# Empty bytes ahead of tiles in a four-layer trunk kernel: where streamed and held rows of matmuls begin modulo 256

## Chip, cores and metric

One core of a Trainium2 chip. The metric is the device time of one execution in microseconds (us), the median of several runs. The trace comes from one profiled execution; its own time and its span (first to last instruction) are given apart.

## The reference

The program is a trunk of four layers on a sequence of 512 tokens with 1024 features, all in float32. Each layer is `x = x + mix(rmsnorm(x))` and then `x = x + ffn(rmsnorm(x))`; a last rmsnorm ends it. The mixers are, in order: an S5 scan with a gated projection (GLU), gated linear attention (GLA), differential attention, and S5 again. In short:

```python
def swiglu_ffn(h, w_gate_up, w_down):
    g, u = jnp.split(h @ w_gate_up, 2, axis=-1)
    return (jax.nn.silu(g) * u) @ w_down          # 1024 -> 2 x 2816 -> 1024
...
    z = jax.nn.gelu(y)                            # end of the S5 mixer
    a, b = jnp.split(z @ w_glu, 2, axis=-1)       # 1024 -> 2 x 1024
    return a * jax.nn.sigmoid(b)
```

GLA and differential attention project `h` with one wide matrix, mix, and project back with `w_o` (1024 x 1024).

## The kernel before

**Products in three passes.** Float32 accuracy is made of float32r matmuls. Each operand is split into a high part (a cast on ACT) and a low part (a subtraction on DVE), which lie side by side in one tile: weights in `whl` (`halves`, L334 and L338), activations in `hT`, `act`, `zT`, `oT`. `mm3` (L351 to L353) issues high x high, high x low and low x high. In the names of the profile, `acc<-whl,act` is a matmul that streams rows of `whl` through the array while a 128x128 block of `act` is held in it; `any<-hT,whl` streams `hT` and holds `whl`. Each matmul has a weight load of its own (the engine row PEld), which brings the next held block while the present one streams.

**Shapes.** There are two shapes of large products. Those of 512 streamed columns are: the FFN's down projection (`gemm_b`; streamed `whl`, held `act`), the GLU (`gemm_b` and `glu` in `s5_pipe`; held `zT`), the projections of the two attentions (held `hT`) and their `w_o` (held `oT`), the scores of the differential attention (L1916; streamed `ks`, held `qs`), and the gate and up products of the first FFN (`gemm_a`; streamed `hT`, held `whl`). Those of 256 columns are the gate and up products of the other three FFNs, done by a Strassen-like scheme of seven products per block (`seven_block`, `seven_product`, L566): the streamed operand is one of seven "sides", sums of quarters of the activations. Two of them ("11" and "12", named `sides` in the profile) lie in the pool `hp`; the other five ("1", "2", "3", "4", "22", named `side`) are opened by `Sides.open` in the FFN's own pool.

**Stages and order.** The start (about 200 us) builds the S5 operators and runs the first S5 scan in a pipe over eight groups, in which DVE, ACT and POOL make operands for TensorE, and a quarter of the GLU's products stands between them. Then FFN, GLA, FFN, differential attention, FFN, S5 with operators spilled to DRAM earlier, and the last FFN. A scheduler orders the instructions by their place in the source, priorities and free buffers; in the attentions and at the start of the Strassen FFNs an order written out by hand is kept.

**Places.** Tiles come from pools that are stacked in each partition's memory, each tile at a multiple of 32 bytes. A pool opened later begins where the long-lived ones end; the last of these is `small` (`self.sp`), eight buffers to each tag, 32 bytes each. So a tile's place depends on every tile allocated under it. The pools of `zT` are on the other side and grow downward from the top.

**The start's norm.** `s5_in` calls `normed` (L443 to L463) for four blocks of 1024 features per row: a square with its sum on ACT into `ms` (L450), an addition on DVE (L437), a power on POOL (`rs`, L439), then the scaling, on ACT and POOL for the first two blocks (L457, L459) and on DVE for the other two (L461). The buffer of the input `xin` is afterwards given to `room`, whose zeros POOL writes (L1103). The same function norms the output at the end.

Of the kernel before, what the change touches and what calls it, by code (L numbers as in the profile page):

```python
# [11 lines left out]
F32 = mybir.dt.float32  # L12
# [9 lines left out]
P = 128  # L22
D = 1024
SEQ = 512
NT = SEQ // P
# [35 lines left out]
class Left:  # L61
# [15 lines left out]
    def room(self):  # L77
        self.hT = [self.tr.hp.tile([P, KT, SEQ], F32R, tag="hT", name=f"hT{z}") for z in range(2)]
# [67 lines left out]
class Sides(Left):  # L146
# [22 lines left out]
        if len(self.heads) == 2:  # L169
            self.total("3")  # L170

    def open(self, pool, names):

        for n in names:
            self.place[n] = pool.tile([P, 2, 4, 256], F32R, name="side" + n)

    def freed(self):
# [85 lines left out]
class Trunk:  # L263
    def __init__(self, ctx, tc, ins, out):
        self.ctx, self.tc, self.nc = ctx, tc, tc.nc
        self.i = ins
        self.out = out
        self.rot = 0
        nc = self.nc
        ep = lambda name, bufs, **k: ctx.enter_context(tc.tile_pool(name=name, bufs=bufs, **k))  # L270
        self.cp = ep("const", 1)
        self.xp = ep("xp", 1)
        self.hp = ep("hp", 2)
        self.wp = ep("wp", 3)
        self.np_ = ep("normp", 2)
        self.sp = ep("small", 8)
        self.ps = ep("psum", 1, space=PSUM)
        self.dp = ep("dram", 1, space=DRAM)
        self.ident = self.cp.tile([P, P], F32, name="ident")
        make_identity(nc, self.ident)  # L280
        self.two_pi = float(np.nextafter(np.float32(TWO_PI), np.float32(0)))
        self.mhalf = self.cp.tile([P, 8], F32, name="mhalf")
        nc.vector.memset(self.mhalf[:], -0.5)
        self.ones = self.cp.tile([P, P], F32, name="ones")
        nc.gpsimd.memset(self.ones[:], 1.0)
        self.dq = nc.sync
        self.jobs = iter(())
        self.pend = []
        self.guard, self.lazy = None, False

    def hand_all(self):
        E = mybir.EngineType
# [149 lines left out]
    def normed(self, xt, g, out, pool, aside=False):  # L442

        nc = self.nc
        if pool is None:
            junk = self.wp.tile([P, D], F32, tag="wst", name="sq", bufs=3)
        else:
            junk = pool.tile([P, D], F32, tag="sq", name="sq", bufs=2)
        ms = self.sp.tile([P, 1], F32, tag="ms", name="ms")
        nc.scalar.activation(junk[:], xt, AF.Square, scale=1.0 / 32.0, accum_out=ms[:])  # L450
        r = self.rsqrt(ms[:], 1, 1e-6)
        if out is None:
            h = pool.tile([P, D], F32, tag="h", name="h", bufs=2)
            nc.vector.scalar_tensor_tensor(h[:], xt, r[:], g[:], op0=ALU.mult, op1=ALU.mult)
            return h
        if aside:
            nc.scalar.mul(junk[:], xt, r[:])  # L457
            gr = lambda y: y.rearrange("p (g c) -> p g c", c=16)
            nc.gpsimd.tensor_tensor(out, gr(junk[:]), gr(g[:]), op=ALU.mult)  # L459
            return  # L460
        nc.vector.scalar_tensor_tensor(  # L461
            out, xt.rearrange("p (g c) -> p g c", c=16), r[:],
            g[:].rearrange("p (g c) -> p g c", c=16), op0=ALU.mult, op1=ALU.mult,  # L463
        )
# [40 lines left out]
    def ffn_plain(self, l, left, after=None, aside=None):  # L505

        nc, i = self.nc, self.i
        wgu, wd = i["ffn_w_gate_up"][l], i["ffn_w_down"][l]
        nxt = None
        with self.tc.tile_pool(name=f"ffn{l}", bufs=1, reuse_waits="tile") as fp:  # L510
            self.jobs = aside(fp) if aside else iter(())
            first = True
            j0 = 0
            for nh in (12, 10):
                acts = []
                for jp in range(j0, j0 + nh, 2):
                    hls, banks = [], []
                    for j in (jp, jp + 1):
                        for half in range(2):
                            hls.append(self.wa(wgu, half * FFN_HIDDEN + j * P))  # L520
                            banks.append(self.anybank())
                            if not first:
                                self.gemm_a(left.hT, hls[-1], banks[-1])
                        if not first:
                            acts.append(self.glu(fp, left.R, banks[-2], banks[-1]))
                            next(self.jobs, None)
                    if first:
                        self.gemm_a4(left, hls, banks)
                        for m in range(2):
                            acts.append(self.glu(fp, left.R, banks[2 * m], banks[2 * m + 1]))  # L530
                        first = False
                        next(self.jobs, None)
                stat = lambda k, part, t: acts[k][:, part, t * P : (t + 1) * P]
                if j0 and after is not None:
                    nxt = Left(self, after)
                for d in range(2):
                    tail = 4 if (d == 1 and j0) else 0
                    self.gemm_b(stat, wd, nh, d * 512, self.add_x(d, nxt, left.r), k0=j0, tail=tail)
                j0 += nh
            for _ in self.jobs:  # L540
                pass
        return nxt
# [169 lines left out]
    def ffn(self, l, left, after=None, turn=False, aside=None):  # L712
# [5 lines left out]
        with self.tc.tile_pool(name=f"ffn{l}", bufs=1, reuse_waits="tile") as fp:  # L718

            room = lambda: fp.tile([P, 2, 4, 256], F32, tag="act", name="lent", bufs=4)  # L720
            left.open(fp, ("1", "2", "4", "3", "22") if l < 3 else ("1", "2"))
            if l == 3:
                lent = room()
            slots = [fp.tile([P, 4, 256], F32, name=f"slot{n}") for n in range(SLOTS)]

            if l < 3:
                lent = room()
            self.jobs = aside(fp) if aside else iter(())
            blocks = [self.seven_block(fp, slots, left, wgu, b, turn) for b in range(FFN_HIDDEN // 256)]
            f = blocks[:2]  # L730
            if l == 3:
                left.open(fp, ("4", "3", "22"))
            for w, n, *room in (
                ("room21", 0), ("room1", 0, lent[:, 0]), ("room21", 1), ("room1", 1, lent[:, 1]), ("room22", 0),
                ("summed", 0), ("summed", 1), ("room22", 1, left.g[:].rearrange("p (k n) -> p k n", n=256)),
# [645 lines left out]
    def s5_first(self, ctx):  # L1381
        nc, i = self.nc, self.i
        xin = self.xp.tile([P, NT, D], F32, tag="x", name="xin")
        zpool = ctx.enter_context(self.tc.tile_pool(name="zT0", bufs=1, side="right"))
        zT = zpool.tile([P, 2, KT, SEQ], F32R, name="zT")
        with self.tc.tile_pool(name="s5_0", bufs=1) as p:
            scr, more = (self.hp.tile([P, 4096], F32, tag="hT", name=f"scr{z}") for z in range(2))
            oms = [more[:, 1024 * z : 1024 * z + 1024].rearrange("p (a b) -> p a b", a=2) for z in range(2)]
# [73 lines left out]
    def s5_second(self, l, ctx, left):  # L1462
        nc = self.nc
        zpool = ctx.enter_context(self.tc.tile_pool(name="zT1", bufs=1, side="right"))
        zT = zpool.tile([P, 2, KT, SEQ], F32R, name="zT")
        with self.tc.tile_pool(name="s5_1", bufs=1) as p:
            room = p.tile([P, 6, 512], F32, name="room2")
            parts = (("in", 0, 2, 2), ("cs", 2, 5, 3), ("out", 5, 8, 2))
            ops = {}

            def get(kk, name):
                if name == "r4":
                    return ops[kk, "cs"][:, 2]
                if name == "map":
                    return ops[kk, "out"][:, 2]
                return ops[kk, name]

            def loads(kk, names):
                for name, a, b, bufs in parts:
                    if name in names:  # L1480
                        o = p.tile([P, b - a, 512], F32, tag=name, name=name, bufs=bufs)
                        nc.sync.dma_start(o[:], self.spill[kk][:, a:b])
                        ops[kk, name] = o

            def steps(kk):
                if kk + 1 < 8:
                    loads(kk + 1, ("in", "cs"))
                if 1 <= kk < 9:
                    loads(kk - 1, ("out",))

            loads(0, ("in", "cs"))
            accs = self.s5_pipe(1, left.hu, zT, False, room, get, steps, left)
        return self.s5_glu(1, zT, accs, self.i["norm_ffn"][l])
# [32 lines left out]
    def gla(self, l, left, after):  # L1526
# [3 lines left out]
        wo = i["gla_w_o"][0]  # L1530
        self.hand(mybir.EngineType.PE)
        with self.tc.tile_pool(name="gla", bufs=1) as p:
            big = lambda name, tag="g8", bufs=5: p.tile([P, 4, 512], F32, tag=tag, name=name, bufs=bufs)
            late = lambda name: big(name, "g8late", 3)
            oT = [p.tile([P, 2, 4, SEQ], F32R, name="oT0"), None]
# [254 lines left out]
    def diff(self, l, left, after):  # L1790
# [2 lines left out]
        w, wo = i["diff_w_qkv"][0], i["diff_w_o"][0]  # L1793
        self.hand(mybir.EngineType.PE)
        with self.tc.tile_pool(name="diff", bufs=1) as p:
            T = lambda tag, bufs=2: p.tile([P, 512], F32, tag=tag, name=tag, bufs=bufs)
            oT = [p.tile([P, 2, 4, SEQ], F32R, name="oT0"), None]
            qks = [p.tile([P, 2, 4, SEQ], F32, tag="qk", name="qk", bufs=2) for _ in range(2)]
# [157 lines left out]

            def normalised(j):
                st, o_s = kept.pop(j)
                q2 = self.sp.tile([P, NT], F32, tag="q2", name="q2")
                v.tensor_tensor(q2[:], st[:, 0], st[:, 0], op=ALU.mult)  # L1960
                v.scalar_tensor_tensor(q2[:], q2[:], 1e-5, st[:, 1], op0=ALU.mult, op1=ALU.add)
                rs = self.rsqrt(q2[:], NT, 0.0)
# [175 lines left out]
```

## Time and profile before

| | before |
|---|---|
| median of 3 runs | 2384.2 us (2383.88 to 2386.3) |
| the profiled execution | 2382.31 us |
| its span | 2380.6 us |
| TensorE busy | 2269.0 us, 95% of the span |
| VectorE (DVE) busy | 1487.1 us, 62% |
| ScalarE (ACT) busy | 1073.0 us, 45% |
| GpSimd (POOL) busy | 266.8 us, 11% |
| read from HBM, written | 275.92 MB, 23.99 MB |
| mean granted clock of TensorE | 0.982 |

A group's row gives line, engine, operation, output and inputs, shapes and count; then busy time in us and mean ns of one; then the idle time ahead of it and what ended that. A busy TensorE is not TensorE at its peak, since a matmul's record reaches from its start to the end of its drain and overlaps the next one. The spacing from one start to the next is what a matmul costs in a row of matmuls.

### The profile page before, as it was taken

The numbers are of one execution on the slowest core, as the hardware profiler recorded it, in microseconds if no ns is written. First come the engines' busy times: TensorE is split into PE (matmuls) and PEld (weight loads), VectorE is DVE, ScalarE is ACT, GpSimd is POOL, SyncE is SP. The second block draws the span as 40 slices with busy tenths as digits, with TensorE's granted clock in tenths as the row PEclk, the third lists the DMA queues.
The fourth block names the chain that finished last, engine by engine and source line by source line (L and its number), as shares of the span: only waits on it lengthen the run. The fifth ranks groups of instructions, "written<-read, shape, count | busy, mean of one in ns | idle before, by whom it ended". The sixth has DMA issues, their size and how long they took to land. (4 is left out here: it accounts for less than half of the span.)

```text
span 2380.6 us, 35208 instructions
## 1 busy us (share of the span) xinstructions
PE 2269.0 (95%) x14055; PEld 1962.8 (82%) x14055; DVE 1487.1 (62%) x2311; ACT 1073.0 (45%) x1749; POOL 266.8 (11%) x335
## 2 busy tenths in 40 slices
PE   4799999999999999999999998989999899999997
PEld 3578888788877789898987887888989788999996
DVE  7774565555443459585753666875847874967674
ACT  4463445444352346252544665653635233634442
POOL 3330100111000011010001221110000000101000
PEclk9699999999999999999999999999999899999999
DMA  4123344544332258564345465694732645666521
GB/s 110 34 52 138 95 138 143 166 129 166 118 103 85 71 143 208 137 177 124 111 142 117 107 133 145 170 243 115 195 98 89 214 158 150 170 179 154 162 76 67
DMA packets 275502, 317.42 MB, mean 133 GB/s; under 512 B 45653, under 2 KB 214377, under 8 KB 274058
## 3 DMA queue, kind: packets, MB, share of 16 engines
q1 hardware_dynamic: 227210, 238.14, 31.9%
q0 software_dynamic: 48128, 77.02, 15.7%
q8 instruction: 111, 1.82, 0.3%
q14 instruction: 53, 0.43, 0.1%
HBM read 275.92 MB, written 23.99 MB: 126 GB/s over the span
## 5 line engine op out<-in xcount | busy, mean ns | idle before, releaser
L338 DVE TENSOR_TENSOR whl<-wst,whl 128x1024 fp32r<-128x1024 f32 x294 | 359.0, 1223 | 363.1 <-ACT whl L334 362.3
L334 ACT CAST whl<-wst 128x1024 fp32r<-128x1024 f32 x294 | 308.4, 1050 | 530.5 <-PE acc L353 354.8
L566 PE MATMUL a<-side,whl 128*128 128x256 f32 x2376 | 291.2, 279 | 14.2 <-ACT r L638 6.0
L566 PEld LDWEIGHTS a<-side,whl 128*128 128x128 f32 x2376 | 281.4, 190 | 16.2 <-ACT whl L334 6.9
L351 PE MATMUL acc<-whl,act 128*128 128x512 f32 x704 | 276.5, 393 | 0.7 <-DVE g L611 0.7
L353 PE MATMUL acc<-whl,act 128*128 128x512 f32 x704 | 276.9, 393 | 0.0
L352 PE MATMUL acc<-whl,act 128*128 128x512 f32 x704 | 275.6, 391 | 0.0
L566 PE MATMUL c<-side,whl 128*128 128x256 f32 x1584 | 192.4, 278 | 3.6 <-DVE whl L338 3.6
L566 PEld LDWEIGHTS c<-side,whl 128*128 128x128 f32 x1584 | 186.9, 189 | 4.0 <-DVE whl L338 4.0
L351 PEld LDWEIGHTS acc<-whl,act 128*128 128x128 f32 x704 | 132.2, 188 | 30.9 <-DVE g L611 1.9
L352 PEld LDWEIGHTS acc<-whl,act 128*128 128x128 f32 x704 | 132.2, 188 | 28.8
L353 PEld LDWEIGHTS acc<-whl,act 128*128 128x128 f32 x704 | 132.3, 188 | 27.9
L351 PE MATMUL any<-hT,whl 128*128 128x512 f32 x384 | 151.7, 395 | 0.0
L352 PE MATMUL any<-hT,whl 128*128 128x512 f32 x384 | 149.6, 390 | 0.0
L353 PE MATMUL any<-hT,whl 128*128 128x512 f32 x384 | 149.6, 389 | 0.0
L351 PE MATMUL acc<-whl,hT 128*128 128x512 f32 x352 | 143.8, 408 | 1.1 <-ACT whl L334 0.6
L352 PE MATMUL acc<-whl,hT 128*128 128x512 f32 x352 | 138.6, 394 | 1.0 <-DVE whl L338 1.0
L353 PE MATMUL acc<-whl,hT 128*128 128x512 f32 x352 | 139.0, 395 | 0.0
L338 DVE TENSOR_TENSOR whl<-halves,whl 128x1024 fp32r<-128x1024 f32 x72 | 87.7, 1222 | 32.5 <-ACT whl L334 32.5
L352 PE MATMUL acc<-whl,zT 128*128 128x512 f32 x256 | 103.9, 406 | 4.1 <-DVE whl L338 4.1
L334 ACT CAST whl<-halves 128x1024 fp32r<-128x1024 f32 x72 | 75.3, 1052 | 69.2 <-PE acc L353 26.7
L351 PE MATMUL acc<-whl,zT 128*128 128x512 f32 x256 | 102.8, 406 | 2.7 <-ACT zT L468 2.7
(438 smaller groups left out, 4185.1 us busy)
## 6 DMA issues: line engine op xcount, KB each, us to landing
wst<-in_ffn_w_gate_up_dram SPq DMA_DIRECT2D x110, 512.0 KB, 4.0
wst<-in_ffn_w_down_dram SPq DMA_DIRECT2D x88, 512.0 KB, 3.7
halves<-in_ffn_w_gate_up_dram SPq DMA_DIRECT2D x42, 512.0 KB, 5.9
slot<-in_ffn_w_gate_up_dram SPq DMA_DIRECT2D x39, 512.0 KB, 6.6
wst<-in_ffn_w_gate_up_dram POOLq DMA_DIRECT2D x33, 512.0 KB, 6.4
wst<-in_s_w_glu_dram SPq DMA_DIRECT2D x32, 512.0 KB, 3.6
spill<-opsp POOLq DMA_DIRECT2D x8, 2048.0 KB, 8.7
wst<-in_gla_w_in_dram SPq DMA_DIRECT2D x24, 512.0 KB, 3.6
```

Source lines behind the costliest of these rows:

```text
L334: self.nc.scalar.copy(hl[:, 0], w[:])
L338: self.nc.vector.tensor_tensor(hl[:, 1], w[:], hl[:, 0].bitcast(F32), op=ALU.subtract)
L351: mm(out, lh, rh, start=first, stop=False)
L352: mm(out, lh, rl, start=False, stop=False)
L353: mm(out, ll, rh, start=False, stop=last)
L566: mm(o, hl[:, x, k, c], side[:, y, k], start=first and not (j or k or n), stop=k == 3 and n == 2, skip_group_check=True,)
```

## The change

A new method `edge` allocates a tile of n bytes that nothing uses. It is called ahead of tiles in the FFN pools, the two attentions, and the pools of `zT`. To make room, two tags of the pool `small` get fewer buffers: `ms` of the plain norm 2 in place of 8, `q2` of the differential attention 6 in place of 8; that pool becomes 256 bytes shorter.

```diff
-    def open(self, pool, names):
+    def open(self, pool, names, edges={}):
         for n in names:
+            self.tr.edge(pool, edges.get(n, 0))
             self.place[n] = pool.tile([P, 2, 4, 256], F32R, name="side" + n)
...
+    def edge(self, pool, n):
+        if n:
+            self.edges += 1
+            pool.tile([P, n // 4], F32, name=f"edge{self.edges}", bufs=1)
...
-        ms = self.sp.tile([P, 1], F32, tag="ms", name="ms")
+        ms = self.sp.tile([P, 1], F32, tag="ms", name="ms", bufs=2)
...
         with self.tc.tile_pool(name=f"ffn{l}", bufs=1, reuse_waits="tile") as fp:   # ffn_plain
+            self.edge(fp, 64)
...
             left.open(fp, ("1", "2", "4", "3", "22") if l < 3 else ("1", "2"))      # ffn
             if l == 3:
+                self.edge(fp, 64)
                 lent = room()
             slots = [fp.tile([P, 4, 256], F32, name=f"slot{n}") for n in range(SLOTS)]
             if l < 3:
+                self.edge(fp, 64)
                 lent = room()
...
             if l == 3:
-                left.open(fp, ("4", "3", "22"))
+                left.open(fp, ("4", "22", "3"), {"4": 32, "22": 32, "3": 128})
...
         zT = zpool.tile([P, 2, KT, SEQ], F32R, name="zT")                           # both S5 layers
+        self.edge(zpool, 32)
...
         with self.tc.tile_pool(name="gla", bufs=1) as p:
+            self.edge(p, 32)
...
         with self.tc.tile_pool(name="diff", bufs=1) as p:
+            self.edge(p, 224)
...
-                q2 = self.sp.tile([P, NT], F32, tag="q2", name="q2")
+                q2 = self.sp.tile([P, NT], F32, tag="q2", name="q2", bufs=6)
```

The places that result, in bytes modulo 256, as the built programs have them. Every float32r product of a group has the same pair, since the steps inside these tiles are multiples of 256 bytes.

| products | columns | count | streamed | held, before | held, after |
|---|---|---|---|---|---|
| FFN down, `acc<-whl,act` | 512 | 2112 | 192 | 128 | 192 |
| GLU, `acc<-whl,zT` | 512 | 768 | 192 | 224 | 192 |
| first FFN gate and up, `any<-hT,whl` | 512 | 1152 | 192 | 192 | 192 |
| attentions' projections, `acc<-whl,hT` | 512 | 1056 | 192 | 192 | 192 |
| GLA `w_o`, `acc<-whl,oT` | 512 | 192 | 192 | 128 | 160 |
| differential attention `w_o`, `acc<-whl,oT` | 512 | 192 | 192 | 128 | 96 |
| its scores, `s<-ks,qs` | 512 | 128 | 192 | 128 | 96 |
| Strassen, sides "11" and "12" | 256 | 1584 | 192 | 192 | 192 |
| Strassen, the other sides | 256 | 3432 | 128 | 192 | 192 |
| last FFN, side "22" | 256 | 264 | 128, after 0 | 192 | 192 |
| last FFN, side "4" | 256 | 264 | 128, after 224 | 192 | 192 |

The order of instructions is the same on TensorE and POOL. On ACT the fourth square of the start's norm moves behind the scaling of the second block and the first cast of `frow`; on DVE the fourth addition (L437) moves between the two scalings of L461, and a few operations of `s5_x` are exchanged; on SP the first loads of GLU weights move behind four copies `bpad<-X` and two loads of `bb`.

More of the change, by code (lines that the diff above doesn't have):

```diff
@@ L267, in __init__ @@
         self.out = out
-        self.rot = 0
+        self.rot = self.edges = 0
         nc = self.nc
@@ L1465, in s5_second @@
         zT = zpool.tile([P, 2, KT, SEQ], F32R, name="zT")
+        self.edge(zpool, 32)
         with self.tc.tile_pool(name="s5_1", bufs=1) as p:
```

## The prediction

> **What bounds the kernel now.** I read the page first: TensorE is busy for 95% of the span, and the idle part lies in the first slices.
>
> ```profile
> span 2380.6 us, 35208 instructions
> PE 2269.0 (95%) x14055; PEld 1962.8 (82%) x14055; DVE 1487.1 (62%) x2311; ACT 1073.0 (45%) x1749; POOL 266.8 (11%) x335
> PE   4799999999999999999999998989999899999997
> ```
>
> The profiled execution took 2382.31 us, 1.7 us more than its span; the median of the runs shown is 2384.2 us (2383.88 to 2386.3). Differences are worked out in the trace and taken off the median. A measurement of this kernel can tell about 0.2% (4.8 us) from no change.
>
> Second, busy time by stage (window, its length, then busy us and count of PE, PEld, DVE, ACT, POOL): the start, the first FFN, the third FFN.
>
> ```profile
> 0.00:200.00 200.00, 145.34 (x1118) 114.50 (x1119) 136.90 (x275) 96.10 (x164) 65.90 (x67) 0.90 0.30 77
> 200.00:680.00 480.00, 479.81 (x2490) 388.41 (x2489) 261.14 (x510) 204.31 (x384) 51.24 (x104) 1.00 0.42 136
> 1500.00:1840.00 340.00, 326.58 (x2327) 305.59 (x2326) 241.86 (x280) 164.50 (x213) 28.34 (x25) 0.98 0.58 155
> ```
>
> After 200 us TensorE hardly stops, while DVE has over a quarter of each window left and the DMA share is 0.42 to 0.58. So a nanosecond off each matmul there reaches the end, until another engine is late. Before 200 us the order of DVE, ACT and POOL counts.
>
> Third, matmuls by line and operand; the last figures are mean ns of one and the idle time before. "acc<-whl,act" streams whl and holds act.
>
> ```profile
> L353 PE MATMUL acc<-whl,act 128*128 128x512 f32 x704 | 276.9, 393 | 0.0
> L351 PE MATMUL acc<-whl,act 128*128 128x512 f32 x704 | 276.5, 393 | 0.7 <-DVE g L611 0.7
> L352 PE MATMUL acc<-whl,act 128*128 128x512 f32 x704 | 275.6, 391 | 0.0
> L352 PE MATMUL acc<-whl,zT 128*128 128x512 f32 x256 | 103.9, 406 | 4.1 <-DVE whl L338 4.1
> L353 PE MATMUL acc<-whl,zT 128*128 128x512 f32 x256 | 103.4, 405 | 1.2 <-DVE zT L469 1.2
> L351 PE MATMUL acc<-whl,zT 128*128 128x512 f32 x256 | 102.8, 406 | 2.7 <-ACT zT L468 2.7
> L566 PE MATMUL a<-side,whl 128*128 128x256 f32 x2376 | 291.2, 279 | 14.2 <-ACT r L638 6.0 <-ACT whl L334 5.9 <-DVE whl L338 2.3
> L566 PE MATMUL c<-side,whl 128*128 128x256 f32 x1584 | 192.4, 278 | 3.6 <-DVE whl L338 3.6
> L566 PE MATMUL a<-sides,whl 128*128 128x256 f32 x792 | 100.3, 283 | 0.0
> L566 PE MATMUL d<-sides,whl 128*128 128x256 f32 x792 | 100.0, 283 | 0.9 <-ACT whl L334 0.9
> ```
>
> These durations overlap, since the next matmul starts before the last has drained. What one costs is the spacing of starts. Fourth, therefore, the timeline of TensorE in stretches without a stop: the first and the 49th start, so 48 spacings, with hT, act and zT held.
>
> ```profile
> 725.87 0.39 PE L351 MATMUL acc<-whl,hT 128*128 128x512 f32 x1
> ...
> 736.75 0.39 PE L351 MATMUL acc<-whl,hT 128*128 128x512 f32 x1
> ```
>
> ```profile
> 1188.20 0.39 PE L351 MATMUL acc<-whl,act 128*128 128x512 f32 x1
> ...
> 1199.19 0.39 PE L351 MATMUL acc<-whl,act 128*128 128x512 f32 x1
> ```
>
> ```profile
> 1954.65 0.40 PE L351 MATMUL acc<-whl,zT 128*128 128x512 f32 x1
> ...
> 1965.85 0.40 PE L351 MATMUL acc<-whl,zT 128*128 128x512 f32 x1
> ```
>
> That is 10.88/48 = 226.7 ns with hT, 10.99/48 = 229.0 ns with act, 11.20/48 = 233.3 ns with zT: same helper, shape and streamed buffers, different held rows. By the table of places, whl begins at 192 modulo 256, hT at 192, act at 128, zT at 224. The equal start has the fastest row.
>
> The 256-column products are otherwise. One row is 24 matmuls:
>
> ```profile
> 1669.56 2.88 PE L566 MATMUL a<-side,whl 128*128 128x256 f32 x24
> 1672.28 3.02 PE L566 MATMUL d<-sides,whl 128*128 128x256 f32 x24
> 1675.14 2.90 PE L566 MATMUL a<-side,whl 128*128 128x256 f32 x24
> ```
>
> From start to start, side (at 128, whl held at 192) takes 2.72/24 = 113.3 ns and sides (at 192, equal) 2.86/24 = 119.2 ns. Here the equal start is the slow one, by 5.9 ns. So the best place depends on the shape; I take each shape's own rows.
>
> **The change, part by part.**
>
> FFN activations: 2112 products go from (192, 128) to equal starts. 229.0 - 226.7 = 2.3 ns, times 2112: **4.8 us less**. They run back to back (0.7 us idle in all), so it reaches the end. What becomes late next is the split of weights: a block of 24 such matmuls lasts 5.5 us and needs one DVE subtraction and one ACT cast, 1.22 and 1.05 us in the rows below, so neither is near.
>
> ```profile
> L338 DVE TENSOR_TENSOR whl<-wst,whl 128x1024 fp32r<-128x1024 f32 x294 | 359.0, 1223 | 363.1 <-ACT whl L334 362.3
> L334 ACT CAST whl<-wst 128x1024 fp32r<-128x1024 f32 x294 | 308.4, 1050 | 530.5 <-PE acc L353 354.8
> ```
>
> GLU: 768 products go from (192, 224) to equal, 233.3 - 226.7 = 6.6 ns each. A quarter (192) is issued inside the S5 pipe, where TensorE waits for other engines; I count that quarter as nothing (up to 1.3 us if it counts). The other 576 give **3.8 us less**.
>
> The two attentions: the w_o products (192 in each) go from held 128 to held 160 and 96, the 128 score products from held 128 to 96. No row shows these pairs. They lose 2.3 ns now, as act does; the bounds are the rows of hT and zT, so -0.9 to +1.7 us for the 384, and for the scores -0.3 to +0.6. The row nearest is the one that they leave, so I take **nothing** and keep -1.2 to +2.3.
>
> Last layer's Strassen sides "22" (264 products, streamed from 128 to 0) and "4" (264, to 224), held at 192. The bounds are the two 256-column rows: 0 to 5.9 ns each, 0 to 3.1 us together; below nothing is excluded, since 113.3 is half of 226.7 and no row of either shape is faster. "22" then lies as far from its held rows (64) as side does now: nothing. "4" lies 32 away, half way between the two rows: 2.95 x 264 = **0.8 us more**.
>
> The smaller pool: the mean squares of the plain norm get 2 buffers instead of 8. The order of instructions is the same on TensorE and POOL; ACT, DVE and SP change places only at the start. This is that place:
>
> ```profile
> 21.72 1.06 ACT L450 ACTIVATE sq<-xin 128x1024 f32<-128x1024 f32 x1 [0.91 <-POOL scr L459]
> 27.33 1.74 POOL L439 TENSOR_TENSOR rs<-ms,mhalf 128x1 f32<-128x1 f32 x1 [5.50 <-DVE ms L437]
> 29.11 1.15 ACT L457 ACTIVATE sq<-xin,rs 128x1024 f32<-128x1024 f32 x1 [2.52 <-POOL rs L439]
> 30.16 1.04 ACT L978 CAST frow<-frow 12x512 fp32r<-12x512 f32 x2
> 32.64 1.08 POOL L439 TENSOR_TENSOR rs<-ms,mhalf 128x1 f32<-128x1 f32 x2
> 33.23 2.48 DVE L461 SCALAR_TENSOR_TENSOR scr<-xin,rs,gain 128x1024 f32<-128x1024 f32 x2 [3.31 <-POOL rs L439]
> 35.77 0.52 POOL L1103 MEMSET room<- 64x512 f32 x1 [2.06 <-DVE scr L461]
> ```
>
> The fourth square (21.72) must now wait until POOL has read the second sum (29.07), and stands between the two casts of frow: about 30.8 to 32.0. Behind it on ACT waits the second cast, over at 32.6 instead of 31.2; its reader comes after the copies into room, which wait for the scaled rows until 35.8, so that is covered. On DVE the fourth mean square now stands between the two scaled rows (L461): the first ends at 34.5, then 0.1 for the sum, one POOL power (1.08/2 = 0.54), the hops between the engines (about 0.2), the second 1.24: 36.6 instead of 35.71. **0.9 us more**, as the room's fills wait for it. Nothing if a later stage absorbs it; 2.1 if that power takes 1.74 as the first row's did. On SP the first two loads of GLU weights move behind four small copies and two loads, from 20.3 to about 29; their first cast comes at 60.52, so that is covered:
>
> ```profile
> 60.52 1.05 ACT L334 CAST whl<-wst 128x1024 fp32r<-128x1024 f32 x1
> ```
>
> The last norm uses the same buffers. Its fourth square would wait about 1 us, while the third and fourth outputs wait for earlier stores anyway:
>
> ```profile
> 2370.49 1.04 ACT L450 ACTIVATE sq<-x 128x1024 f32<-128x1024 f32 x1
> 2370.82 0.55 POOL L439 TENSOR_TENSOR rs<-ms,mhalf 128x1 f32<-128x1 f32 x1 [1.47 <-DVE ms L437]
> 2375.44 1.29 DVE L454 SCALAR_TENSOR_TENSOR h<-x,rs,gain 128x1024 f32<-128x1024 f32 x1 [0.20 <-DMA out_dram<-h]
> ```
>
> Square at 2371.4 to 2372.7, sum and power by 2373.5: before 2375.44, so nothing.
>
> Sum: -4.8 - 3.8 + 0.8 + 0.9 = **-6.9 us**, from 2384.2 to 2377.3 (the profiled execution to 2375.4).
>
> **The rivals.**
>
> *Places do not matter.* What differs between the rows would be something else about the tiles, and only the prologue's 0.9 us remains: 2385.1 us. Against it: side and sides run from the same line in the same block and differ by 5.9 ns per matmul. For it: every pair of rows differs in its tile's pool too, not in the place alone. This is also what the Trainium skill would say: "SBUF — State Buffer", section "SBUF: two separate sides", names only the port pair shared by DVE and GpSimd as contended on the engines' side, lets TensorE wait for nobody, and gives it a second, independent read port for the weight load. By that rule the sum is the prologue alone; the 226.7, 229.0 and 233.3 ns above do not agree with it as it stands. Chance 0.10.
>
> *Given back by the new places.* The moved Strassen sides cost 5.9 ns each (+3.1), the attentions stand like zT (+2.3) and the prologue costs 2.1: -8.6 + 7.5 = -1.1, 2383.1 us. The profile has no row for those pairs, which is all that speaks for it; against it, all of them would have to fall badly. Chance 0.17.
>
> *Slower: the equal start is what costs.* The 256-column rows show 5.9 ns for it. If act and zT behave so when aligned, 226.7 + 5.9 = 232.6 ns: act +3.6 x 2112 = +7.6 us, GLU -0.7 x 576 = -0.4, with the 0.8 and 0.9 above +8.9: 2393.1 us. It decides from the point where the aligned product takes 2.6 ns over 226.7 ((4.8 + 3.8 - 1.7) / 2688). Against it stands the hT row: the same code, aligned, at 226.7 in a long stretch. Chance 0.06.
>
> **How the numbers follow.** The forecast has 0.67. Low end: gains with the pipe's quarter and the attentions' best, without any cost: -8.6 - 1.3 - 1.2 = -11.1, 2373.1 us. High end: the case of places that don't matter, 2385.1, which includes the case given back (2383.1). Outside are the slower rival and a little of each side, under 0.2. Faster by over 0.2% is below 2379.4: most of the forecast, 0.61. Slower by over 0.2%, above 2389.0: the slower rival and little else, 0.07. Within: 0.32.
>
> **What would show it.** Means of the act rows near 389 and starts 10.88 us apart over 48 products; the same for GLU's products outside the pipe. Products with "4" and "22" in the last layer at 2.72 to 2.86 us per 24. The second L461 ending at 36.6 us. Wrong if act does not fall below 229 ns, if another engine's waits grow by what TensorE saves, or if the start is later by over 2 us.

## The result and the profile after

The changed kernel takes 2393.92 us (median of 5 runs, 2392.09 to 2395.46) against 2384.2 us for the kernel before in the same series: ratio 1.0035, 95% interval 1.0019 to 1.0051. It is slower, where 2377.3 us was forecast. The profiled execution took 2395.39 us.

The page's first lines after:

```profile
span 2393.7 us, 35209 instructions
PE 2271.2 (95%) x14055; PEld 1968.1 (82%) x14055; DVE 1486.5 (62%) x2311; ACT 1072.3 (45%) x1749; POOL 267.6 (11%) x335
```

TensorE's share says nothing: 95% both times. Its matmuls by line do (mean ns, then idle time):

```profile
L358 PE MATMUL acc<-whl,act 128*128 128x512 f32 x704 | 276.0, 392 | 0.1
L359 PE MATMUL acc<-whl,act 128*128 128x512 f32 x704 | 274.4, 390 | 0.0
L360 PE MATMUL acc<-whl,act 128*128 128x512 f32 x704 | 274.3, 390 | 0.0
L359 PE MATMUL acc<-whl,zT 128*128 128x512 f32 x256 | 102.6, 401 | 4.2 <-DVE whl L345 4.2
L574 PE MATMUL a<-side,whl 128*128 128x256 f32 x2376 | 297.3, 282 | 16.2 <-ACT r L646 6.2
L574 PE MATMUL c<-side,whl 128*128 128x256 f32 x1584 | 193.7, 279 | 7.0 <-ACT whl L341 4.9
```

(L351 to L353 are L358 to L360 now, L566 is L574.) The aligned rows are shorter: `act` 390 to 392 where it had 391 to 393, `zT` 401 where it had 405 or 406. The rows of `side`, whose products were mostly not touched, are longer, and the idle time ahead of `c<-side` went from 3.6 to 7.0 us. In starts over 48 spacings, first `act`, then `zT`:

```profile
1195.59 0.39 PE L358 MATMUL acc<-whl,act 128*128 128x512 f32 x1
...
1206.47 0.39 PE L358 MATMUL acc<-whl,act 128*128 128x512 f32 x1
```

```profile
1968.21 0.39 PE L358 MATMUL acc<-whl,zT 128*128 128x512 f32 x1
...
1979.09 0.39 PE L358 MATMUL acc<-whl,zT 128*128 128x512 f32 x1
```

Both take 10.88/48 = 226.7 ns, exactly the row of `hT` that the forecast was made from. So the gain came. To find the loss, the start of each TensorE instruction is taken from its start in the trace before (both issue the same 14055 in one order). Later is positive, in us:

| place in the trace before | 190 | 700 | 760 | 870 | 930 | 1290 | 1345 | 1500 | 1960 | 2110 | 2350 |
|---|---|---|---|---|---|---|---|---|---|---|---|
| after | 0.5 | -2.0 | -0.4 | 0.2 | **11.3** | 7.5 | 13.8 | 15.2 | 14.1 | 13.0 | 13.2 |

It falls wherever `zT` and `act` are held (190 to 700, 930 to 1290, 1500 to 2010), and rises by 11 us within 60 us: the start of the second FFN, 870 to 930. The windows there (columns as in the prediction; the last three are the granted clock of TensorE, the busy share of the DMA engines and their GB/s), the kernel before first:

```profile
850.00:875.00 25.00, 24.22 (x119) 20.11 (x119) 12.75 (x18) 10.46 (x22) 4.85 (x4) 1.00 0.75 142
890.00:895.00 5.00, 5.00 (x47) 5.00 (x46) 4.48 (x8) 1.83 (x3) 1.11 (x1) 1.00 0.68 103
895.00:930.00 35.00, 30.96 (x261) 29.93 (x260) 31.78 (x39) 22.39 (x29) 5.16 (x4) 1.00 0.81 204
```

```profile
850.00:875.00 25.00, 24.24 (x117) 19.88 (x118) 12.63 (x18) 10.12 (x21) 0.00 (x0) 1.00 0.00 0
890.00:895.00 5.00, 0.68 (x2) 0.50 (x2) 1.92 (x2) 1.77 (x2) 1.94 (x3) 0.80 1.18 238
895.00:930.00 35.00, 31.09 (x226) 30.37 (x226) 29.25 (x35) 19.16 (x25) 5.89 (x5) 0.84 1.01 238
```

The last three columns tell it. Before, the DMA engines moved 142 GB/s in the 25 us up to 875; after, nothing at all; then the loads come all together, and TensorE issues 2 matmuls in 5 us and goes on at a granted clock of 0.84. What held the loads back stands in the waits of SP's queue between 780 and 900 us (line, what it waited for, us, times, longest), before and after:

```profile
SPq L599 <- DVE hh L86: 22.2, 1, 22.2
```

```profile
SPq L607 <- PE acc L360: 35.9, 1, 35.9
```

These are each kernel's longest wait of line L599, now L607, which loads weights into the slots and into `lent`. Before, it is a later load, behind the slots' (issued at 877.95); after, it is the first load into slot 0, as the timeline of the queue shows, before and after:

```profile
841.16 0.46 SPq L599 DMA_DIRECT2D slot<-in_ffn_w_gate_up_dram  x1
841.67 0.50 SPq L599 DMA_DIRECT2D lent<-in_ffn_w_gate_up_dram  x1
```

```profile
840.47 0.37 SPq L331 DMA_DIRECT2D wst<-in_ffn_w_gate_up_dram  x1
876.74 0.37 SPq L607 DMA_DIRECT2D slot<-in_ffn_w_gate_up_dram  x1
877.16 0.50 SPq L607 DMA_DIRECT2D lent<-in_ffn_w_gate_up_dram  x1
```

The first load of the FFN's weights into slot 0 is issued 36 us later. It waits for a matmul of L360 in the stage before, GLA's `w_o`, which holds `oT`. Why can be read from the bytes. Before, slot 0 began at 173952, where a tile of 8 KB ended that held the second half of `oT` (`oT1` in the program). After, the smaller pool moved both down by 256; then GLA's edge of 32 bytes moved `oT1` up to an end of 173728, while the FFN's edge stands behind its slots, so slot 0 begins at 173696. The two overlap by 32 bytes, and a load may not overwrite what a matmul has yet to read.

### The profile page after: what moved, and what is told of

It is laid out like the page before. It is cut to its first block, busy times and chain, and to the rows that moved or that the text cites. A ratio compares the mean times of both kernels' runs of the same rounds, so it can differ in the third digit from the quotient of the medians.

```text
span 2393.7 us, 35209 instructions
## 1 busy us (share of the span) xinstructions
PE 2271.2 (95%) x14055; PEld 1968.1 (82%) x14055; DVE 1486.5 (62%) x2311; ACT 1072.3 (45%) x1749; POOL 267.6 (11%) x335
## 5 line engine op out<-in xcount | busy, mean ns | idle before, releaser
L574 PE MATMUL a<-side,whl 128*128 128x256 f32 x2376 | 297.3, 282 | 16.2 <-ACT r L646 6.2
L574 PEld LDWEIGHTS a<-side,whl 128*128 128x128 f32 x2376 | 287.1, 193 | 18.3 <-ACT whl L341 7.0
L358 PE MATMUL acc<-whl,act 128*128 128x512 f32 x704 | 276.0, 392 | 0.1
L360 PE MATMUL acc<-whl,act 128*128 128x512 f32 x704 | 274.3, 390 | 0.0
L574 PE MATMUL c<-side,whl 128*128 128x256 f32 x1584 | 193.7, 279 | 7.0 <-ACT whl L341 4.9
L574 PEld LDWEIGHTS c<-side,whl 128*128 128x128 f32 x1584 | 188.0, 190 | 7.7 <-ACT whl L341 5.1
L358 PEld LDWEIGHTS acc<-whl,act 128*128 128x128 f32 x704 | 132.1, 188 | 28.9 <-DVE g L619 0.8
L360 PEld LDWEIGHTS acc<-whl,act 128*128 128x128 f32 x704 | 132.1, 188 | 27.7
L358 PE MATMUL any<-hT,whl 128*128 128x512 f32 x384 | 151.7, 395 | 0.0
L360 PE MATMUL any<-hT,whl 128*128 128x512 f32 x384 | 149.6, 390 | 0.0
L358 PE MATMUL acc<-whl,hT 128*128 128x512 f32 x352 | 144.3, 410 | 1.1 <-ACT whl L341 0.6
L360 PE MATMUL acc<-whl,hT 128*128 128x512 f32 x352 | 139.0, 395 | 0.0
L358 PE MATMUL acc<-whl,zT 128*128 128x512 f32 x256 | 101.6, 401 | 2.7 <-ACT zT L475 2.7
```

Of the source, the lines that this page charges most:

```text
L358: mm(out, lh, rh, start=first, stop=False)
L360: mm(out, ll, rh, start=False, stop=last)
L574: mm(o, hl[:, x, k, c], side[:, y, k], start=first and not (j or k or n), stop=k == 3 and n == 2, skip_group_check=True,)
```

## The experiments

All ratios are to the kernel before, run beside them. Runs of one kernel spread by up to 15 us, so the interval is what to go by.

**1. The FFN's edge ahead of its slots.** All places modulo 256 of the 512-column products stay; slot 0 begins at 173760, past the end of `oT1`.

```diff
+            if l < 3:
+                self.edge(fp, 64)
             slots = [...]
             if l < 3:
-                self.edge(fp, 64)
                 lent = room()
```

> The changed kernel, with the 64 empty bytes of the second and third FFN ahead of the three slots instead of behind them. Every pair of streamed and held rows stays as in the changed kernel. Theory of the overlap: slot 0 begins 32 bytes inside the last tile of the linear attention's pool, so its load, and all loads behind it on SP, wait for the attention's last product; with the bytes ahead of the slots it no longer does. Then 10 to 12 us less than the changed kernel, 2382 to 2384 us, and the first slot load is issued near 840 us of the span again. Rival, slower loads (the transfers or their queue suffer from the moved places): the load is late here too, within 2 us of 2393.9.

Measured: 2383.53 us, ratio 0.9991 (0.9978 to 1.0003). The first slot load is issued early again, and between 870 and 930 us nothing is lost (0.0 and 0.1 in the measure of the table):

```profile
840.72 0.46 SPq L607 DMA_DIRECT2D slot<-in_ffn_w_gate_up_dram  x1
```

Moving 64 empty bytes from behind the slots to ahead of them is worth 1.0035 - 0.9991 = 0.0044, some 10 us. The rest of the change is then within 0.2% of nothing: beside its gain a smaller loss is left.

**2 and 3. One attention's edge left out.** Without GLA's, `oT1` ends where slot 0 begins; without the differential attention's, the overlap stays.

```diff
         with self.tc.tile_pool(name="gla", bufs=1) as p:
-            self.edge(p, 32)
```

> The changed kernel without the 32 empty bytes of the linear attention. Theory of the overlap: the attention's pool then ends where slot 0 begins, and the stall goes as in the run before; its w_o products go back to held 128, 0.7 us less. 2381 to 2384 us. Rival, slower loads: only the 0.7 us, 2393.

```diff
         with self.tc.tile_pool(name="diff", bufs=1) as p:
-            self.edge(p, 224)
```

> The changed kernel without the 224 empty bytes of the differential attention. One theory: the stop of TensorE by some 5 us near 1315 us comes from the attention's own moved places (its copies of hl, its scores) and goes: 5 to 7 us less, 2387 to 2389. Rival: it comes from the times at which loads and copies meet on the DMA engines and has nothing to do with the places; then 0.7 us less by the w_o products, and the stop stays or moves, 2391 to 2394.

Measured: without GLA's edge 2383.65 us, 0.9993 (0.9976 to 1.001), slot load at 840.48; without the other 2392.61 us, 1.0032 (1.0019 to 1.0045), slot load at 875.18 and 11.0 us lost between 870 and 930. Only the first takes the loss away. The second came out as its rival had it (2391 to 2394 us): that edge is not worth the 5 to 7 us that the other theory put on it.

**4. The kernel before with GLA's edge alone.** Nothing else of the change is in it.

> The kernel before with nothing but the 32 empty bytes of the linear attention. Theory of the overlap: its last tile then ends 32 bytes inside slot 0 of the next FFN, and the stall of 9 to 12 us is there alone: 2393 to 2396 us. Rival, slower loads or another part of the change: 0.7 us more by the w_o products held at 160, 2385.

Measured: 2399.49 us (5 runs), 1.0063 (1.0041 to 1.0086). The same wait stands alone, and 10.2 us are lost between 870 and 930:

```profile
SPq L605 <- PE acc L359: 35.9, 1, 35.9
```

With the experiments before, this shows the cause: 32 bytes of overlap, made by one edge, whatever places the rest has. The time is above the 2393 to 2396 us that were expected; the rest of the 15 us lies outside 870 to 930. The profiled execution, the slowest of the five (2404.62 us), has a slow stretch near 145 us (told below) of some 5 us; how much of the median that explains is open.

**5. Every pair equal, no overlap.** The first experiment, with edges of 64 in both attentions (held `oT` and `qs` at 192) and the last layer's sides back at 128.

```diff
-            self.edge(p, 32)      # gla
+            self.edge(p, 64)
...
-            self.edge(p, 224)     # diff
+            self.edge(p, 64)
...
-                left.open(fp, ("4", "22", "3"), {"4": 32, "22": 32, "3": 128})
+                left.open(fp, ("4", "3", "22"), {"4": 192})
```

> The kernel after with four edges changed: the FFN's edge ahead of its slots in the first three layers (slot 0 begins where GLA's last tile ends), both attentions' edge 64 (their held rows then begin at 192 modulo 256, as whl), and the last layer's sides 4, 22 and 3 back at 128. Theory A, places act on each matmul as the spacings of the kernel after show, and the overlap of slot 0 was the large loss: against the same kernel with only the first of these edits (2383.5 us) the 384 products with oT fall from 233.3 to 227.3 ns (-2.3 us), the 128 score products likewise (-0.8), sides 22 and 4 from 117.9 and 116.8 to 114.0 ns for 264 each (-1.8): 2378.6 us, ratio 0.9977 to the kernel before, oT and score spacings within 1 ns of 227.3. Theory B, what a place saves there is taken back by waits for loads and copies: spacings fall but the time stays at 2383.5, ratio 0.999. If the spacing of oT stays above 231 ns at equal starts, places modulo 256 are not what sets it.

Measured: 2378.64 us, 0.9971 (0.996 to 0.9983). Theory A, by the time. The steady spacings (stops of over 300 ns left out) of `oT` fell from 233.4 to 228.7 ns in GLA and from 233.3 to 228.2 in the other attention, those of sides "22" and "4" from 117.9 and 116.8 to 113.4 and 113.3. The scores did not follow: expected within 1 ns of 227.3, they went from 233.4 to 232.2. They come in rows of four with a stop behind the first, so few of their spacings are steady.

**6. The aligned products and the smaller pool alone.** No edge in the attentions, last layer's sides at 128.

> The kernel after without the edges of the two attentions and with the last layer's sides at 128: the FFN's and GLU's equal starts and the smaller pool are left; slot 0 begins at 173696, which is where GLA's last tile ends when GLA has no edge, so there is no overlap. Theory A (my prediction's first two terms were right and the losses came from the overlap and the new places): -4.0 for act and -3.4 for zT by the measured spacings, +0.5 for the start: 2384.2 - 6.9 = 2377.3 us, ratio 0.997; first slot load of the second FFN issued near 840 us. Theory B (the gains in TensorE's pace are lost again in the stops near 1310 us and at the second FFN's start, whatever the places): 2382 to 2384 us, ratio 0.999 to 1.000.

Measured: 2379.64 us, 0.9966 (0.9954 to 0.9979), that is 8.1 us less (5.0 to 11.0). Theory A: what the forecast counted as gains was there in full.

**7. The smaller pool alone, in the kernel before.**

> The kernel before with the smaller pool alone: 2 buffers for the mean squares and 6 for q2; all later tiles then lie 256 bytes lower, at the same place modulo 256. Prediction's term: +0.9 us, 2385.1, ratio 1.0004, second scaled row ending at 36.6 us from the start in place of 35.7. What the kernel after showed: +0.4 to +0.5, ratio 1.0002. Rival: the pool costs more than its place in the start shows, since everything behind it meets at other times: +4 us or more, ratio above 1.0015, with a later offset of TensorE that begins in the first 100 us and stays.

Measured: 2390.42 us, 1.0017 (1.0003 to 1.0031). By the interval it costs 0.7 to 7.4 us; its place at the start shows +0.4 (at 100 us of the profiled execution). Of the 10.2 us that this profile is late in the end, 5.2 come between 1290 and 1345 us and 4.7 in one piece at 143 us:

```profile
140.00:145.00 5.00, 4.14 (x24) 2.63 (x25) 5.00 (x5) 3.50 (x7) 3.35 (x2) 0.74 0.21 40
145.00:150.00 5.00, 5.00 (x20) 4.03 (x20) 1.53 (x2) 1.98 (x4) 0.10 (x1) 0.50 0.02 3
150.00:155.00 5.00, 5.00 (x30) 4.82 (x30) 1.54 (x3) 2.83 (x4) 0.00 (x0) 0.73 0.01 1
```

The kernel before in its second of these windows:

```profile
145.00:150.00 5.00, 5.00 (x40) 4.78 (x40) 2.63 (x6) 4.08 (x6) 0.10 (x1) 1.00 0.05 10
```

TensorE is busy throughout in both, with twenty matmuls against forty at a granted clock of 0.50 against 1.00. Experiments 4 and 5 have this stretch too (4.8 and 4.6 us lost between 140 and 150), 1 to 3 and 6 not; the kernel after has it in its second profile (4.6, below) and not in its first. So it comes and goes between executions.

**8. Sides "11" and "12" as well.** As 5, with these two 192 bytes further on in a longer tile, at 128 like the other sides; `rs`, `ms2`, `sums` and `nm` get 4 buffers each for room.

> As the first of these runs, and sides 11 and 12 of the 256-column products in the first Strassen layers begin 192 bytes further on in a tile that is 256 bytes longer, at 128 modulo 256 as the other sides (streamed 64 below the held whl); rs, ms2, sums and nm get 4 buffers in place of 8 to make the room. Theory A: 1584 products fall from 119.5 to 113.8 ns: -9.0 us against the first run, to about 2369.6, if another engine isn't late. Theory A with a limit: DVE or ACT is late by half of it, -4.5, 2374. Theory B, the pace of sides is not of their place (they hold other rows, stand elsewhere in the block): the spacing stays at 119.5 and the time at the first run's. If the smaller buffers make waits in the attentions, their spans grow there and the saving is that much less.

Measured: 2387.63 us, 1.0005 (0.999 to 1.0019): 9 us slower than 5, where 4.5 to 9 us less was expected. Both theories fall. Two stretches of its profile, of products at the same pair of places:

```profile
904.20 5.60 PE L574 MATMUL c<-side,whl 128*128 128x256 f32 x48
...
918.35 2.88 PE L574 MATMUL a<-sides,whl 128*128 128x256 f32 x24
921.07 0.39 PE L574 MATMUL c<-side,whl 128*128 128x256 f32 x2
```

```profile
1067.37 2.99 PE L574 MATMUL a<-side,whl 128*128 128x256 f32 x24
1070.20 2.99 PE L574 MATMUL d<-sides,whl 128*128 128x256 f32 x24
1073.03 2.99 PE L574 MATMUL a<-side,whl 128*128 128x256 f32 x24
```

At 918 a row of 24 takes 2.72 us (113.3 ns each), at 1067 every row takes 2.83 (117.8 ns). It stays at one of the two for tens of us: most rows run at 113.3 ns up to 960 us, all of them at 117.8 from 1002 to 1185. A pair of places allows more than one pace, and something else chooses. Over the whole profile "11" and "12" fell from 119.4 to 116.7 ns (1584 products, -4.2 us against 5) and the other five rose from 113.7 to 116.4 (3960, +10.8). These 6.6 us are most of the 9, though the profiled execution was the fastest of the twelve (2379.47 us).

**9. Side "11" alone.** As 8, with "12" back at 192.

> As the run in which sides 11 and 12 both began at 128 modulo 256, but side 12 alone goes back to 192, the equal start; 11 stays at 128. In that run every 256-column product ran either at 113.3 or at 117.8 ns for tens of us on end, with the same places throughout; with 11 and 12 at the equal start the others return to 113.3 within four products after each row of 12 and stay. Theory C, the pace is a state that lasts until something resets it, and the row at the equal start is what resets it: the sides at 128 stay at 113.3 to 113.8, 11 comes down from 119.5 to about 113.6, 792 x 5.9 ns = -4.7 us against the run with all places equal and no overlap: 2378.6 - 4.7 = 2374, ratio 0.9952. Theory D, the longer tile, the shift of all later tiles by 512 bytes or the smaller buffers made the pace of 117.8 in that run: it is there again, about 2386.

Measured: 2377.91 us, 0.9963 (0.9949 to 0.9976). The time lies between theory C (2374) and theory D (2386). The pace agrees with C: row "12" of the block at the equal start takes 2.86 us, and the rows around it are back at 2.72.

```profile
1062.35 2.88 PE L574 MATMUL a<-sides,whl 128*128 128x256 f32 x24
1065.07 2.88 PE L574 MATMUL c<-side,whl 128*128 128x256 f32 x24
1067.79 2.88 PE L574 MATMUL a<-side,whl 128*128 128x256 f32 x24
1070.51 3.02 PE L574 MATMUL d<-sides,whl 128*128 128x256 f32 x24
1073.37 2.90 PE L574 MATMUL a<-side,whl 128*128 128x256 f32 x24
```

"11" fell from 119.3 to 114.3 ns (-4.0 us over 792), but the other five, 3960 products, rose from 113.7 to 114.0 (+1.3): about -2.7 us of the expected -4.7. Against run 5 the interval can't tell that from nothing.

**10. Run 5 with 8 buffers for the mean squares.** Room from `sums` (6) and `nm` (4), places unchanged.

> The run with all places equal and no overlap (2378.6), but the mean squares keep their 8 buffers and the room comes from sums (6 buffers in place of 8) and nm (4 in place of 8), so that no place changes. Theory that the smaller pool of mean squares itself costs time (the kernel before with it alone was at 1.0017 of before): -1 to -4 us, 2374.6 to 2377.6, ratio near 0.9955. Rival, its cost is the +0.4 seen at the start and the rest of the 1.0017 was the scatter of clock dips that differ from execution to execution: within 0.1% of 2378.6. If sums and nm make waits in the second attention, its span of 1220 to 1500 us grows.

Measured: 2378.74 us, 0.9963 (0.9948 to 0.9978). Beside 0.9971 of run 5 that is -0.0008, with intervals of 0.0030 and 0.0023. Neither theory is excluded; whether the smaller pool makes the stretch at 143 us likelier stays open.

**11. Both.** Side "11" at 128 and 8 buffers for the mean squares.

> Side 11 alone at 128 and the mean squares with 8 buffers; the room comes from sums, nm (3 buffers each), st and q2 (5 each), rs and ms2 (4 each). The sum of the two runs before it: by theory C with no price of the pool 2374, ratio 0.995; with the pool's price taken away as well 2370 to 2373, ratio 0.9935 to 0.995. If the cut buffers make the second attention wait, that shows between 1220 and 1500 us and is taken off.

Measured: 2376.32 us, 0.9958 (0.9943 to 0.9973), the fastest version, 0.4% under the kernel before, but not the 2370 to 2374 that was expected. The difference to 5, 9 and 10 is within the intervals.

**12. After once more**, beside 9 to 11.

> The kernel after itself, unchanged, beside the others on one chip. Overlap theory with the places' small losses: ratio 1.002 to 1.005 as in the result, and 12 us over the run with all places equal and no overlap; the stop of 5 us near 889 us is there in its profile again, with the first slot load of the second FFN issued near 876 us. If that stop were a chance of one execution, the profile wouldn't show it again.

Measured: 2393.05 us, 1.0026 (1.0016 to 1.0037), and the same wait in its profile:

```profile
SPq L607 <- PE acc L360: 35.9, 1, 35.9
```

## Why the prediction was wrong

- **FFN activations, -4.8 us: right in mechanism, a fifth too large.** Over all steady pairs the spacing went from 229.0 to 227.2 ns: 2112 x 1.8 = 3.8 us less.
- **GLU, -3.8 us: right.** 233.1 to 227.7 ns: 576 x 5.4 = 3.1 us less. The quarter in the pipe brought nothing, as forecast: in the trace after, TensorE is 0.4 us late at its first product and 0.4 behind its last, and 14.3 and 14.2 in the second S5. Experiment 6 gives the sum of both and of the start as -8.1 (5.0 to 11.0); forecast -7.7.
- **Attentions, 0: inside the bounds (-1.2 to +2.3), the chosen value wrong.** `oT` went from 229.6 to 233.4 and 233.3 ns: 384 x 3.7 = +1.4, and +0.2 for the scores. The value was taken from the row that they left; held 32 below the streamed start and 96 below it are both as slow as 32 above it. The scores were not losing 2.3 ns as `act` did, which the forecast took: before, they were spaced by 232.1 ns at the same pair of places.
- **Sides "22" and "4", +0.8: "4" nearly right, "22" wrong.** These are the rows of "4" and "22", and the start of the next:

```profile
2180.80 2.96 PE L574 MATMUL c<-side,whl 128*128 128x256 f32 x24
2183.60 2.99 PE L574 MATMUL a<-side,whl 128*128 128x256 f32 x24
2186.43 3.04 PE L574 MATMUL a<-sides,whl 128*128 128x256 f32 x24
```

"4" takes 2.80 us, between 2.72 and 2.86 as forecast; "22" 2.83, not 2.72. Being as far above its held rows as `side` lies below them is not the same. Against the same rows before (113.3 and 113.4 ns) that is 264 x (3.5 + 4.5) = +2.1.

- **Smaller pool, +0.9: the step right, its reach half.** The second scaling ends at 36.59, as worked out (36.6):

```profile
33.29 1.28 DVE L468 SCALAR_TENSOR_TENSOR scr<-xin,rs,gain 128x1024 f32<-128x1024 f32 x1 [3.17 <-POOL rs L446]
...
35.30 1.29 DVE L468 SCALAR_TENSOR_TENSOR scr<-xin,rs,gain 128x1024 f32<-128x1024 f32 x1 [0.46 <-POOL rs L446]
```

TensorE is 0.9 us late at 40 us and 0.5 at 190. Experiment 7 leaves 0.7 to 7.4 us for the whole of it.

- **The step that failed: "ACT, DVE and SP change places only at the start", and with it that nothing else waits.** The prediction goes by the order of instructions and by the places modulo 256. It does not ask which earlier tile each moved tile now lies on, and its sum has no term for a load that must wait. SP's order is the same near 840 us, but one load in it gained a wait of 35.9 us, the loads queued behind it came late with it, and TensorE stopped for 4.86 us and ran on at the lower clock:

```profile
883.12 6.34 PE L574 MATMUL d<-sides,whl 128*128 128x256 f32 x48
894.32 0.80 PE L574 MATMUL c<-side,whl 128*128 128x256 f32 x2 [4.86 <-ACT whl L341]
```

That is +11.1 us between 870 and 930: the stop, and by an estimate some 5.6 us for 35 us at a clock of 0.84 (the window above). With it the measured terms are -3.8 - 3.1 + 1.6 + 2.1 + 0.5 + 11.1 = +8.4 us; the ratios of the two series give +8.3 and +6.2. That they meet so closely is in part luck, since both profiled executions are 13 us late in the end.

The rivals: "Places do not matter" falls with experiment 6; the rule of the Trainium skill beside it ("SBUF — State Buffer", section "SBUF: two separate sides": TensorE waits for nobody) names nothing that would make 226.7 and 233.3 ns of one line, which the rows above show. "Given back by the new places" had a part (+3.7 of its +5.4). The slower rival was the wrong mechanism: equal starts took 226.7 ns, not 232.6. That its time, 2393.1 us, lies 0.8 us from the measured one is chance. That another engine's waits may grow by what TensorE saves was named among what would make it wrong, without a place or a price.

The trace after also loses 6.3 us between 1290 and 1345 (differential attention). This is not put down to the change: the kernel before with the smaller pool alone, with no edge in that attention, lost 5.2 there, experiment 6 (no edge there either) 5.9, experiment 4 (the old pool) 4.7, the kernel without GLA's edge but with that one 0.7, and the kernel with every pair equal 2.4. What makes it is open.

## What to carry to other kernels

Empty bytes in one stacked pool move every tile's end as well as its start: after such a change compare, tile by tile, which earlier tile's memory each one takes over and who reads that last, since here 32 shared bytes made a load wait for that reader, with all that was queued behind. Put the padding where ends of earlier and starts of later tiles keep their order. Take a spacing for a pair of places only from rows of that pair, and where paces last for long stretches, measure a whole stage.

## What the runs showed of the hardware

Mean spacing of float32r matmuls in steady rows, by where the held rows begin against the streamed ones (modulo 256):

| columns | held against streamed | ns |
|---|---|---|
| 512 | equal | 226.7 to 228.7 |
| 512 | 64 below | 229.0 to 229.7 |
| 512 | 32 below, 96 below | 233.4, 233.3 |
| 512 | 32 above | 233.1 |
| 256 | 64 above | 113.3, or 117.8 for long stretches |
| 256 | 32 below | 116.8 |
| 256 | 64 below (192 above) | 117.9 |
| 256 | equal | 119.4 |

The scores are not in this table: at equal starts, at 64 below and at 96 below their few steady spacings have means of 232.2, 232.1 and 233.4 ns.

The two paces of one pair were not expected. In the kernel after, and in experiments 5 and 6, a row at 64 above, in the blocks behind the first two, reaches 113.3 ns within four products behind a row at the equal start; with no such row, in experiment 8, stretches of 80 us on end stay at 117.8. So the equal row may be what resets the pace, but it does not do so each time. In the kernel before, behind the rows of `act`, a row of "11" at the equal start is followed by two rows of 2.83 us, and only behind "12" do they take 2.74 and then 2.72 (start and length in us, from the chain that ended last):

```profile
1766.61 2.88 PE a L566 x24
1769.50 2.83 PE c L566 x24
1772.33 2.83 PE a L566 x24
1775.15 2.87 PE d L566 x24
1778.03 2.74 PE a L566 x24
```

What sets the pace was not found.

The stretches of half the clock are the other surprise: one kernel has them in one profiled execution and not in another. That near 143 us cost 4.7 us in experiment 7, begins behind a wait of TensorE of 1 us and lasts 10 us; the kernel before has the same wait (1.03 us ahead of 140.25) and not the stretch. The clock goes with much of the spread between runs: over the 34 runs of the kernel before beside experiments 5 to 8 the mean granted clock lies between 0.978 and 0.986, and a run is on average 1.3 us shorter for each 0.001 of it (correlation -0.72). The Trainium skill, "TensorE: Matmul & The Clock Gate", section "Part 1: The HAM clock gate (the "warmup" mystery)", says that the gate leaves the clock either half or full, and that a free-running window of activity sets it. The 0.50 and 1.00 of the windows above agree, values between them being means over a window; that the phase of the gate's own window decides is not shown by any run here.
